# Modulation products of a two-layer attention block: two weight pieces at a time, four chunks of features in four column groups

## The chip, the cores and the metric

One core of one Trainium2 chip runs the whole program. The metric is the time of one execution on the device in microseconds; the kernel before took 3713.2 us, the median of 3 runs (3712.51 to 3716.09).

## The reference, cut to what matters

The reference is two attention layers over 512 tokens and 256 context tokens, followed by two larger blocks (feed-forward, a mixer, cross-attention, feed-forward). Each of the two attention layers scales, shifts and gates its tokens by a modulation, which depends on one vector `c` for the tokens and one, `c_ctx`, for the context:

```python
def _layer(x, ctx, c, c_ctx, w_ada, b_ada, norm_g, w_in, ...):
    mod_x = jax.nn.silu(c) @ w_ada + b_ada
    shift_x, scale_x, gate_x = jnp.split(mod_x[:, None, :], 3, axis=-1)
    mod_c = jax.nn.silu(c_ctx) @ w_ada + b_ada
    shift_c, scale_c, gate_c = jnp.split(mod_c, 3)
    hx = _rmsnorm(x, norm_g) * (1.0 + scale_x) + shift_x
    hc = _rmsnorm(ctx, norm_g) * (1.0 + scale_c) + shift_c
    ...
    x_new = x + gate_x * out_x
```

Here `w_ada` is 1024 x 3072 per layer in float32, and the two vectors are two rows: a product with a large weight (12.6 MB per layer) and almost nothing on the other side.

## The kernel before, in words

**The work as a whole.** `model` (line 1955) runs a start stage, the first block with its two layers (`Block1.run`), and then the second block. Most matrix products are carried in three passes of split weights: `Net.weight` (line 117) loads a piece of 128 x 1024 (512 KB) into a tile `ws`, ScalarE rounds it into `wh` (line 114), VectorE takes the rest into `wl` (line 115), and `mm3` (line 127) issues three matmuls per chunk, on lines 131 to 133. The tiles `wh` come from a ring of four buffers, `whi`.

**The modulation** is `Start.ada`, lines 226 to 258. A layer's 3072 columns are worked in six sixths of 512. For a sixth `g` the 1024 features are eight chunks of 128, which lie in four pieces of the weight with two chunks each. A piece is loaded by SP's queue (line 234) directly into a buffer of the ring `whi`, unsplit, since these products run in plain float32 (two passes per product). Its two products (line 237) follow at once. Each product has the 32 columns of `sT` (of which two, `c` and `c_ctx`, are not zero) as the stationary operand and 512 columns of the weight as the moving one; its 32 output rows lie at `r = 64 * (q % 2) + 32 * k` of one PSUM bank, so that the chunks 0 to 3 go to the four column groups of the array, and chunks 4 to 7 are added to them. ScalarE copies the bank out (line 242); four small matmuls with a selector (line 246) add the four groups and put the features on partitions; VectorE adds the bias (line 248). The function is a generator: it yields after each of the first three pieces, after the copy and after the selector step, five steps per sixth.

**Who calls it, and when.** In `model`, `weave` (line 1964) spreads 20 steps of the first four sixths of layer 0 over 20 rounds, with 10 steps of the memory's keys and values and 20 of the loads of tokens. There the scheduler of the framework places TensorE's instructions. When they are there, `modulated` (line 403) applies scale and shift to the normed tokens, half of the chunks on POOL and half on VectorE (line 418), and the projections of the first unit follow. The other eight sixths (two of layer 0, six of layer 1) are woven into the attention of layer 0: `attend` (line 996) takes one step of `ada` after each block of the attention (line 1021). Two units of neighbourhood attention have 20 blocks each, which makes the 40 steps. The order of TensorE's instructions is that of the code in this part (`manual_schedule`, line 1048). SP's queue issues in order, too: a load that waits for its buffer holds up what stands behind it, such as the exchanged keys `kB` (line 488) and the relative biases `nbase` (line 646).

**What else runs there.** The blocks' own matmuls are scores (lines 493, 494), transposes (722, 552), sums (519) and the preparation of the next head (478). In between comes the fill, `zgate` (line 874), whose two weight pieces stay in use until its last step; `attention` (line 563) spreads its steps over the blocks.

Of the kernel before, what the change touches and what calls it, by code (L numbers as in the profile page):

```python
# [15 lines left out]
P = 128  # L16
# [13 lines left out]
# column ranges of w_in of the first block  # L30
# [3 lines left out]
# column ranges of the table of constants  # L34
# [14 lines left out]
# columns of the packed vectors: vectors of 128 n features as n columns  # L49
# [11 lines left out]
class Net:  # L61
    """Shared pools and building blocks.

    Matrix products with float32 operands are carried by three float32r passes: an operand a is
    hi + lo, hi its rounding to float32r and lo the exact rest, and a*b = hi*hi + hi*lo + lo*hi.
    """
# [12 lines left out]
    # -- allocation ------------------------------------------------------------------------------  # L79
    def psum(self, tag="ps"):  # L80
        """A bank of PSUM; tag: products (ps: p3 and p1), scores (pS), transposes (pT), weighted sums (po), or any (None)."""
        if tag is None:
            tag = ("p3", "pS", "p3", "pT", "p3", "pS", "p1", "po")[self.nps % 8]
            self.nps += 1
        elif tag == "ps":
            tag = ("p3", "p3", "p3", "p1")[self.nprod % 4]
            self.nprod += 1
        return self.pp.tile([P, 512], F32, name=tag, tag=tag, bufs=dict(p3=3, p1=1, pS=2, pT=1, po=1)[tag])
# [4 lines left out]
    # -- constants -------------------------------------------------------------------------------  # L93
# [12 lines left out]
    def bcast_row(self, ap, n, name, pool=None):  # L106
        """A vector of DRAM on every partition."""
        t = (pool or self.cp).tile([P, n], F32, name=name, tag=name)
        self.nc.sync.dma_start(t, ap.partition_broadcast(P))
        return t  # L110

    # -- splitting -------------------------------------------------------------------------------
# [4 lines left out]
    def weight(self, src, nk, eng=None):  # L117
        """A piece of a weight, packed as [128, nk * w], as (hi, lo) of [128, nk, w]."""
# [8 lines left out]
    def mm3(self, pt, items, first=True, last=True):  # L127
        """pt += sum of stationary.T @ moving over items (sh, sl, mh, ml)."""
# [6 lines left out]
    # -- small vectors ---------------------------------------------------------------------------  # L135
# [3 lines left out]
    def rsqrt(self, src, n, mul, add, bufs=3):  # L139
        """1 / sqrt(src * mul + add) of [128, n], by Newton's method."""  # L140
# [17 lines left out]
    def rows(self, r, ts, out, tag="ps"):  # L158
        """out[:, i*128 + t] = r[t, ts[i]] on every partition."""
# [7 lines left out]
def drain(gen):  # L167
    """The rest of a generator."""
    for _ in gen:
        pass  # L170


def during(gen, extra):
    """The steps of a generator, with something more done at some of them."""
    for i, _ in enumerate(gen):
        if extra.get(i):
            extra[i]()
        yield


def weave(gens):
    """Generators in turn, each with its number of steps, spread over the whole."""
# [14 lines left out]
def between(a, b, n):  # L197
    """The steps of a, n of b after each, then the rest of b."""
# [6 lines left out]
class Start:  # L205
    """What does not depend on x: the modulations and the memory's keys and values."""
# [11 lines left out]
    def silu_c(self):  # L218
        net, nc = self.net, self.net.nc
        # c and c_ctx as 2 of 32 columns  # L220
# [5 lines left out]
    def ada(self, l, g0=0, g1=6):  # L226
        """Sixths of the shift, scale and gate of layer l, each with its feature on a partition; a step for each piece of the weight."""
        net, nc = self.net, self.net.nc
        mod, b = self.mod[l], net.col["b_ada"][:, 24 * l:24 * l + 24]
        for g in range(g0, g1):  # L230
            ps = net.psum("p1")
            for q in range(4):
                w = net.whi.tile([P, 1024], F32R, name="wh", tag="wh").bitcast(F32)
                nc.sync.dma_start(w, net.I["w_ada"][l, g, q])
                for k in range(2):
                    r = 64 * (q % 2) + 32 * k
                    nc.tensor.matmul(ps[r:r + 32, :], self.sT[:, 2 * q + k, :], w[:, k * 512:k * 512 + 512],
                                     start=q < 2, stop=q >= 2)
                if q < 3:
                    yield  # L240
# [17 lines left out]
    def memory(self, pool):  # L258
        """The memory with features on partitions and 1/rms of its tokens, on partitions and along rows."""
# [23 lines left out]
    def gained(self, l, hi, lo, mem):  # L283
        """A chunk of the memory times its gains of layer l's norm, as (hi, lo)."""
# [8 lines left out]
    def keys(self, l, hi, lo, put, n):  # L293
        """The memory's keys of layer l; a step for n chunks of features."""
# [12 lines left out]
    def values(self, l, hi, lo, put, n):  # L307
        """The memory's values of layer l; a step for n products of a piece of the weight."""
# [14 lines left out]
    def first(self, pool):  # L323
        """The memory; keys and values of the first layer, in steps."""
# [20 lines left out]
        def normed():  # L345
            """The normed memory, for the second layer."""
# [7 lines left out]
    def second(self, hi, lo, keys, put, n):  # L354
        """Keys or values of the second layer, in steps; hi, lo: four tiles each of 512 columns."""
# [12 lines left out]
class Block1:  # L368
    """Neighbourhood and grouped attention over tokens in the order (column, row), context tokens last."""
# [9 lines left out]
    # -- the modulated norm ----------------------------------------------------------------------  # L379
    def square(self, x, c, acc, pool):  # L380
        """acc += x_c ** 2."""
# [9 lines left out]
    def rms(self, acc, n, pool):  # L391
        """1/rms of each token, along rows."""
# [10 lines left out]
    def modulated(self, xs, l, i, rb=None):  # L403
        """Scale and shift of the normed tokens (i = 0) or of the context (i = 1), as (hi, lo); rb where xs are not normed."""
# [18 lines left out]
    def tok(self, t, pieces, ps, k0=0, k1=8):  # L423
        """ps = hx[token tile t] @ 256 columns, of it the features k0 .. k1."""
# [12 lines left out]
    # -- heads -----------------------------------------------------------------------------------  # L437
    def head_norm(self, ps, out):
        """out = ps / rms of each head of 64; ps and out [128, 2, heads * 64] of two token tiles."""
# [12 lines left out]
    def rope(self, x, nh, t, tabs):  # L452
        """x = x * C + swapped halves of x * S, for token tiles t and t + 1."""
# [12 lines left out]
    def stacked(self, src, nt, name, st):  # L466
        """[hi; lo] on the partitions by tokens, of one head's src [128, nt, 64] (tokens on partitions)."""
# [14 lines left out]
    def keys(self, src, st):  # L482
        """kA: the keys' [hi; lo], kB: its halves exchanged."""
# [12 lines left out]
    def evac(self, dst, src):  # L496
        """A copy out of PSUM, by both engines in turn."""
# [6 lines left out]
    def normed(self, p, sums):  # L504
        """p times half of 1 / sums."""
# [5 lines left out]
    def room(self):  # L511
        """Room for the transposed weights of a pair of query blocks."""
        return self.bq.tile([P, NT * L], F32, name="wT", tag="wT", bufs=2)

    def sums(self, ps, parts):
        """ps[0:64] + ps[64:128] = sum of V.T @ weights over parts (V, weights), keys on partitions."""
# [4 lines left out]
    def result(self, ps, i, at, o):  # L521
        """The sums of head i of a unit, to its rows of o."""
# [5 lines left out]
    def ctx_queries(self, st, keys, vs, i, n, o):  # L528
        """Stages of the context queries, on the context keys alone."""
# [33 lines left out]
    def attention(self, heads, fill, done, lag, steps, last):  # L563
        """A unit's heads, each (its preparation, its blocks), the first prepared.

        The transposes of a block's weights come lag steps after its scores, its sums one more; the preparation of the
        next head and the fill run in between.
        """
# [3 lines left out]
        # steps of the fill after each block, more of them where nothing is prepared  # L572
# [25 lines left out]
    # -- neighbourhood attention -----------------------------------------------------------------  # L598
    def bank(self):
        """Banks of the projections in turn."""  # L600
# [3 lines left out]
    def na_proj(self, l, u, out):  # L604
        """Keys, queries and values of four heads; a step for each token tile."""
# [7 lines left out]
        def pairs(w, ts, dst, gain=None):  # L613
            """The normed heads of token tiles, two at a time."""
# [26 lines left out]
    def na_base(self, l, u):  # L641
        """Relative biases of four heads: query (cq, rq) on a partition, key (j, rk)."""
# [7 lines left out]
    def na_bias(self, base):  # L650
        """Negated relative bias, for the first, the inner and the last query blocks, then zeros for the context."""
# [11 lines left out]
    def unit_out(self):  # L663
        """The tile of a unit's heads, there from its first use on."""
# [8 lines left out]
    def na_unit(self, l, u, d):  # L673
        """The heads of a unit and what is left to do after them."""
# [6 lines left out]
    def na_head(self, l, i, nq, d, base, o):  # L681
# [26 lines left out]
        def parts(b):  # L708
            """(columns of the weights, V) of the block's keys, 128 at a time, then 64."""
# [34 lines left out]
    # -- grouped attention -----------------------------------------------------------------------  # L744
    def gqa_tables(self, l):
        """Rotary tables with the gains, for queries (with the negated scale) and keys."""
# [19 lines left out]
    def normed_rope(self, ps, nh, t, n, x):  # L766
        """The normed and turned heads of token tiles t and t + 1."""
# [9 lines left out]
    def gqa_proj(self, l, g, out):  # L777
        """Queries of four heads and, of both groups, keys and values; a step for each token tile."""
# [30 lines left out]
    def gqa_unit(self, l, g, d):  # L809
        """The heads of a unit and what is left to do after them."""  # L810
# [58 lines left out]
    # -- gates, output, residual -----------------------------------------------------------------  # L869
    def units(self, d, l, u):  # L870
        """Unit u of a layer's scratch in DRAM: [128, 256 * token tiles]."""
        return d[l].rearrange("p (u c) -> p u c", u=4)[:, u, :256 * (NT if l == 0 else 4)]

    def zgate(self, l, u):
        """z * (1 + tanh(z / 2)), twice silu(z), of a unit; four steps for a token tile."""
# [22 lines left out]
    def gate(self, l, u, o, z):  # L898
        """The unit's attention times its gate, to DRAM."""
# [5 lines left out]
    def early_gate(self, l, j):  # L905
        """Chunk j of the gates, to DRAM; a step for each chunk of features."""
# [13 lines left out]
    def gated(self, l, u, n_):  # L920
        """The unit's gated attention with features on partitions: two chunks of (hi, lo)."""
# [1195 lines left out]
```

## Time and profile before

| | |
|---|---|
| median of 3 runs | 3713.2 us (3712.51 to 3716.09) |
| span of the profiled execution | 3715.2 us |
| TensorE matmul busy | 3618.4 us, 97% |
| TensorE weight loads busy | 2996.4 us, 81% |
| VectorE, ScalarE, GpSimd busy | 2070.7, 1375.2, 762.7 us |
| moved by DMA | 364.35 MB, mean 98 GB/s |
| loads of the modulation weight | 48 of 512 KB |

The profile is one execution. PE stands for TensorE's matmuls, PEld for its weight loads, DVE, ACT, POOL and SP (SPq: its queue) for the vector, scalar, GpSimd and sync engines. An entry such as `L237` is a line of the kernel; `p<-wh,sT` names the tile written and the tiles read. Matmuls are pipelined, so the duration of one overlaps the next; the distance between starts tells what an instruction holds up. A bracket at the end of a timeline row is the time that the engine was idle before it, and what ended the wait. Times count from the start of the span.

### The profile page before, as it was taken

To read this page: it belongs to the slowest core of one execution; us is meant where nothing else is said; L and a number is where in the kernel's file an instruction comes from. 1 tells how busy PE (TensorE), PEld (TensorE's weight loads), DVE (VectorE), ACT (ScalarE), POOL (GpSimd) and SP (SyncE) were. 2 spreads that over 40 slices of the span, in tenths; PEclk is the share of its full clock that TensorE was granted. 3 is DMA by queue.
4 is the path that set the end of the run, shared out by engine and by line. 5 is a ranking of instruction groups with operands and counts; after the bars stand their busy time and mean duration, and the time that the engine had idled before them with its cause. 6 is when DMAs were issued, how large, how long until landed. Compare 5 with 4: busy or idle time off the path is not lost.

```text
span 3715.2 us, 51467 instructions
## 1 busy us (share of the span) xinstructions
PE 3618.4 (97%) x19706; PEld 2996.4 (81%) x19706; DVE 2070.7 (56%) x4209; ACT 1375.2 (37%) x2407; POOL 762.7 (21%) x908
## 2 busy tenths in 40 slices
PE   8999999999999999999999999999999999999998
PEld 6887778888887778888778888888888888788887
DVE  6665763376566464334766433443347887664335
ACT  4334443233345432223654322322233333443223
POOL 1222330032233011102320100210025444101001
PEclk9999999999999999999999999999999999999999
DMA  8434113143322333333122333333333212322333
GB/s 276 128 111 136 58 49 128 63 142 88 88 70 67 139 100 102 97 94 105 58 91 63 108 97 97 97 97 97 97 100 112 57 56 74 115 75 93 101 98 103
DMA packets 135718, 364.35 MB, mean 98 GB/s; under 512 B 30000, under 2 KB 43184, under 8 KB 134960
## 3 DMA queue, kind: packets, MB, share of 16 engines
q1 hardware_dynamic: 135472, 361.06, 31.2%
q8 instruction: 155, 2.54, 0.3%
q14 instruction: 91, 0.75, 0.1%
HBM read 331.64 MB, written 19.66 MB: 95 GB/s over the span
## 4 chain that ended last, share of the span: by engine, by line
PE 87%; DVE 6%; ACT 2%; DMA 2%; issue 1%; POOL 1%; SPq 0%; DVEq 0%; ACTq 0%; POOLq 0%
PE p L131 15%; PE p L133 15%; PE p L132 15%; PE pS L131 7%; PE pS L132 6%; PE pS L133 6%; PE po L519 2%; PE pT L132 2%; PE pT L131 2%; PE pT L133 2%; PE po L132 2%; PE po L131 2%; PE po L133 2%; DVE wl L115 1%; PE pS L493 1%
## 5 line engine op out<-in xcount | busy, mean ns | idle before, releaser
L114 ACT ACTIVATE wh<-ws 128x1024 fp32r<-128x1024 f32 (+4 forms) x561 | 563.7, 1006 | 1421.8 <-PE p L132 683.8
L115 DVE TENSOR_TENSOR wl<-ws,wh 128x1024 fp32r<-128x1024 f32 (+3 forms) x542 | 640.4, 1182 | 252.7 <-ACT wh L114 250.8
L131 PE MATMUL p<-nh,wh 128*128 128x512 f32 x1084 | 429.1, 397 | 4.5 <-ACT nh L1132 2.0
L133 PE MATMUL p<-nh,wl 128*128 128x512 f32 x1084 | 424.7, 392 | 4.7 <-DVE wl L115 4.7
L132 PE MATMUL p<-nl,wh 128*128 128x512 f32 x1084 | 424.2, 391 | 1.9 <-DVE nl L115 1.9
L1199 POOL TENSOR_TENSOR g<-g,rb 128x512 f32<-128x512 f32 x88 | 149.8, 1704 | 1137.1 <-ACT g L1198 1137.1
L131 PE MATMUL pS<-nh,wh 128*128 128x512 f32 x620 | 254.5, 411 | 1.0 <-DVE xr L1182 1.0
L133 PEld LDWEIGHTS p<-nh,wl 128*128 128x128 f32 x1084 | 203.5, 188 | 50.3 <-DVE wl L115 6.2
L133 PE MATMUL pS<-nh,wl 128*128 128x512 f32 x620 | 242.8, 392 | 0.0
L132 PE MATMUL pS<-nl,wh 128*128 128x512 f32 x620 | 242.6, 391 | 0.0
L131 PEld LDWEIGHTS p<-nh,wh 128*128 128x128 f32 x1084 | 203.6, 188 | 46.8 <-ACT nh L1132 2.5
L132 PEld LDWEIGHTS p<-nl,wh 128*128 128x128 f32 x1084 | 203.7, 188 | 42.2 <-DVE nl L115 2.2
L1197 DVE TENSOR_TENSOR g<-p,rb 128x512 f32<-128x512 f32 x88 | 60.4, 691 | 227.8 <-PE p L133 217.6
L131 PE MATMUL p<-hxh,wh 128*128 128x512 f32 (+1 forms) x456 | 183.9, 403 | 0.8 <-DVE wT L502 0.8
L132 PE MATMUL p<-hl,wh 128*128 128x512 f32 (+1 forms) x488 | 179.8, 369 | 0.0
L133 PE MATMUL p<-hh,wl 128*128 128x512 f32 (+1 forms) x488 | 179.4, 368 | 0.0
L131 PE MATMUL p<-hh,wh 128*128 128x512 f32 (+1 forms) x488 | 179.3, 368 | 0.0
L1141 POOL TENSOR_TENSOR acc<-acc,sq 128x512 f32<-128x512 f32 x48 | 73.5, 1532 | 477.4 <-ACT sq L1140 477.0
L133 PE MATMUL p<-hxh,wl 128*128 128x512 f32 (+1 forms) x456 | 170.5, 374 | 0.0
L132 PE MATMUL p<-hxl,wh 128*128 128x512 f32 (+1 forms) x456 | 170.5, 374 | 0.0
L509 POOL TENSOR_SCALAR p<-p,rinv 128x768 f32<-128x768 f32 (+2 forms) x128 | 104.3, 815 | 254.0 <-DVE rinv L508 145.7
L1212 DVE SCALAR_TENSOR_TENSOR xr<-p,xr 128x512 f32<-128x512 f32 (+1 forms) x68 | 42.5, 627 | 170.0 <-PE p L133 169.9
(592 smaller groups left out, 8864.2 us busy)
## 6 DMA issues: line engine op xcount, KB each, us to landing
ws<-in_ffn_w_in_dram SPq DMA_DIRECT2D x176, 512.0 KB
ws<-in_ffn_w_out_dram SPq DMA_DIRECT2D x64, 512.0 KB
ws<-in_w_in_tok_dram SPq DMA_DIRECT2D x52, 512.0 KB
wh<-in_w_ada_dram SPq DMA_DIRECT2D x48, 512.0 KB
ws<-in_ffn_w_out_dram SPq DMA_DIRECT2D x40, 384.0 KB
ws<-in_w_out_dram SPq DMA_DIRECT2D x24, 512.0 KB
ws<-in_dn_qkv_dram SPq DMA_DIRECT2D x24, 512.0 KB
ws<-in_xa_wk_dram SPq DMA_DIRECT2D x16, 512.0 KB
```

Of the source, the lines that this page charges most:

```text
L114: self.last_hi = self.nc.scalar.activation(hi, src, AF.Copy)
L115: (eng or self.nc.vector).tensor_tensor(out=lo, in0=src, in1=hi.bitcast(F32), op=OP.subtract)
L131: mm(pt, sh, mh, start=first and i == 0, stop=False)
L132: mm(pt, sh, ml, start=False, stop=False)
L133: mm(pt, sl, mh, start=False, stop=last and i == n - 1)
L493: mm(ps, q, kA[:, k0:k1], start=True, stop=False)
L509: nc.gpsimd.tensor_scalar(p, p, r, 0.5, op0=OP.mult, op1=OP.mult)
L519: self.net.nc.tensor.matmul(ps[h:h + HD, :], v, w, start=i < 2, stop=i >= len(parts) - 2)
L1141: (nc.vector if c == 7 else nc.gpsimd).tensor_tensor(out=acc, in0=acc, in1=sq, op=OP.add)
L1197: nc.vector.tensor_tensor(t, pg, self.rb, op=OP.mult)
L1199: nc.gpsimd.tensor_tensor(out=t, in0=t, in1=self.rb, op=OP.mult)
L1212: nc.vector.scalar_tensor_tensor(x, ps, 0.5, x, op0=OP.mult, op1=OP.add)
```

## The change

The loop over the four pieces of a sixth becomes one over two halves. A half takes two buffers of the ring, loads two pieces, and issues its four products one behind the other, each to a column group of its own. A sixth has three steps where it had five, and the number of steps in the start stage's `weave` follows. All other lines differ only in comments.

```diff
         for g in range(g0, g1):
             ps = net.psum("p1")
-            for q in range(4):
-                w = net.whi.tile([P, 1024], F32R, name="wh", tag="wh").bitcast(F32)
-                nc.sync.dma_start(w, net.I["w_ada"][l, g, q])
-                for k in range(2):
-                    r = 64 * (q % 2) + 32 * k
-                    nc.tensor.matmul(ps[r:r + 32, :], self.sT[:, 2 * q + k, :], w[:, k * 512:k * 512 + 512],
-                                     start=q < 2, stop=q >= 2)
-                if q < 3:
+            for h in range(2):
+                ws = []
+                for q in (2 * h, 2 * h + 1):
+                    ws.append(net.whi.tile([P, 1024], F32R, name="wh", tag="wh").bitcast(F32))
+                    nc.sync.dma_start(ws[-1], net.I["w_ada"][l, g, q])
+
+                for i in range(4):
+                    nc.tensor.matmul(ps[32 * i:32 * i + 32, :], self.sT[:, 4 * h + i, :],
+                                     ws[i // 2][:, i % 2 * 512:i % 2 * 512 + 512], start=h == 0, stop=h == 1)
+                if h == 0:
                     yield
             y = net.sm.tile([P, 512], F32, name="yada", tag="yada", bufs=1)
             nc.scalar.activation(y, ps, AF.Copy)
...
-            drain(weave([(st.ada(0, 0, 4), 20), (chain(keys, islice(values, 2)), 10), (b1.first(pool), 20)]))
+            drain(weave([(st.ada(0, 0, 4), 12), (chain(keys, islice(values, 2)), 10), (b1.first(pool), 20)]))
```

## Rows read from the trace of the kernel before

**Rows 1.** The page: the span, and TensorE's busy time, share, instructions.
```profile
span 3715.2 us, 51467 instructions
PE 3618.4 (97%) x19706; PEld 2996.4 (81%) x19706; DVE 2070.7 (56%) x4209; ACT 1375.2 (37%) x2407; POOL 762.7 (21%) x908
```

**Rows 2.** The line of the modulation products: duration min/median/max in ns, first and last start.
```profile
L237 PE MATMUL p<-wh,sT x192: 592/605/1061, 13.2 to 353.9; 128*32 128x512 f32 x192
```

**Rows 3.** Windows (length, busy us and instructions per engine, PEclk, DMA share, GB/s).
```profile
10.00:30.00 20.00, 18.18 (x100) 14.23 (x101) 12.52 (x31) 10.98 (x21) 0.00 (x0) 1.00 1.00 376
...
160.00:226.00 66.00, 65.05 (x458) 42.57 (x456) 39.09 (x107) 34.57 (x82) 25.56 (x46) 1.00 0.53 154
...
292.00:358.00 66.00, 64.82 (x459) 42.45 (x458) 39.14 (x106) 33.36 (x83) 21.89 (x40) 1.00 0.50 146
```

**Rows 4.** Timeline of TensorE in the first attention stretch (start, duration, line, tiles).
```profile
162.42 1.05 PE L237 MATMUL p<-wh,sT 128*32 128x512 f32 x4
...
177.76 1.05 PE L237 MATMUL p<-wh,sT 128*32 128x512 f32 x4
178.74 0.38 PE L493 MATMUL pS<-kA,qA 128*128 128x256 f32 x1
...
181.35 1.05 PE L237 MATMUL p<-wh,sT 128*32 128x512 f32 x4
...
222.08 1.05 PE L237 MATMUL p<-wh,sT 128*32 128x512 f32 x4
```

**Rows 5.** Timeline of TensorE in the start stage, where visits stand together.
```profile
53.18 1.06 PE L237 MATMUL p<-wh,sT 128*32 128x512 f32 x8
54.18 0.39 PE L131 MATMUL p<-mh,wh 128*128 128x256 f32 x1
...
66.05 1.91 PE L237 MATMUL p<-wh,sT 128*32 128x512 f32 x12
```

**Rows 6.** Timeline of SP's queue: loads of the modulation weight, and kB's transfers.
```profile
166.07 0.33 SPq L234 DMA_DIRECT2D wh<-in_w_ada_dram  x1
...
178.85 0.33 SPq L234 DMA_DIRECT2D wh<-in_w_ada_dram  x1
...
297.24 0.33 SPq L234 DMA_DIRECT2D wh<-in_w_ada_dram  x1
297.67 1.11 SPq L488 DMA_DIRECT2D kB<-kA  x2
```

**Rows 7.** Waits of SP's queue, 155 to 230 us: total, times, longest.
```profile
SPq L234 <- PE p L237: 30.4, 10, 7.9
```

**Rows 8.** Timeline of TensorE: visits that waited for their load.
```profile
171.01 1.05 PE L237 MATMUL p<-wh,sT 128*32 128x512 f32 x4 [0.87 <-DMA wh<-in_w_ada_dram]
...
302.41 1.05 PE L237 MATMUL p<-wh,sT 128*32 128x512 f32 x4 [1.10 <-DMA wh<-in_w_ada_dram]
```

**Rows 9.** Two 512 KB loads alone: SP's queue, then windows (last two columns: DMA).
```profile
2830.20 0.81 SPq L121 DMA_DIRECT2D ws<-in_dn_qkv_dram  x2
...
2833.00:2834.00 1.00, 0.01 (x1) 0.01 (x1) 0.84 (x2) 0.12 (x1) 0.88 (x3) 1.00 0.99 406
...
2834.30:2834.60 0.30, 0.30 (x5) 0.30 (x4) 0.24 (x1) 0.00 (x0) 0.22 (x2) 1.00 0.17 68
2834.60:2835.00 0.40, 0.40 (x4) 0.31 (x3) 0.31 (x1) 0.00 (x0) 0.32 (x2) 1.00 0.00 0
```

**Rows 10.** Waits of TensorE in layer 1's neighbourhood attention, 880 to 1060 us.
```profile
PE pS L494 <- DMA kB<-kA: 7.8, 4, 2.4
```

**Rows 11.** A gap on TensorE in layer 1, and the window behind it.
```profile
890.88 0.33 PE L494 MATMUL pS<-kB,qA 128*128 128x192 f32 x1 [1.74 <-DMA kB<-kA]
...
891.30:894.60 3.30, 3.30 (x13) 2.62 (x11) 0.80 (x3) 1.69 (x3) 1.49 (x3) 0.50 0.03 5
```

**Rows 12.** The end of the start stage: POOL's scaling, TensorE's first projection.
```profile
83.59 12.51 POOL L418 TENSOR_SCALAR x<-x,modA,mod 128x512 f32<-128x512 f32 x8
...
98.48 0.58 PE L131 MATMUL pS<-wh,hxh 128*128 128x256 f32 x1 [6.59 <-ACT vo L342]
```

## The prediction

> **What bounds the kernel now.** I read the page first: matmuls are busy 97% of the span [rows 1], so a microsecond taken from TensorE is worth a microsecond wherever it does not have to wait for something else there. The change touches only the modulation products, so I asked next where those stand. The line of their matmuls has 192 records between 13.2 and 353.9 us [rows 2]. In the timeline they come in groups of four records (two products, each two passes), so there are 48 visits: four for each of 12 sixths, 16 of them in the start stage (to about 74 us) and 32 in the neighbourhood attention of the first layer, in two stretches of 16. In those two stretches TensorE is busy 65.05 and 64.82 of 66 us [rows 3]: there it is the bound, and it works in the order in which the code lists its instructions. In the start stage it shares that place with the loads: from 10 to 30 us the DMA engines are busy without a pause at 376 GB/s [rows 3]. Third, I looked at what happens around one visit, on TensorE and on the queue that issues its loads.
>
> **What the change takes away.** A visit holds TensorE from 177.76 to 178.74, 0.98 us to the start of the next instruction [rows 4]. Whether four column groups really run at once need not be guessed: at 53.18 us two visits with different column groups happen to stand together, eight records, and the next instruction starts at 54.18, after 1.00 us [rows 5]. So the second pair of column groups is free, and each merged visit saves one whole visit. Twelve records that fall on the same groups again took 1.91 us [rows 5], so the saving needs different groups, which the new loop gives. Attention: 16 visits go, and with 0.06 us each for the slower first instruction behind a visit that is 16 x 1.04 = 16.6 us. Start stage: 8 go, of which two were already merged with a neighbour in rows 5, so 6 x 1.04 = 6.2 us at most. The eviction, the small products with the selector and the DVE additions are as many as before: nothing.
>
> **What it adds: the loads lose their lead.** A visit's piece goes into a buffer of the ring of four that the split weights also use. In the attention stretches two of the four hold the two pieces of z's weight until the stretch is nearly over (the fill runs through every block), so two are left. The trace shows that they are all there is: the load issued at 178.85 goes out 1.09 us after the visit that began at 177.76, when its buffer came free [rows 4, 6], and the queue spent 30.4 us in one stretch, 10 times, waiting for these matmuls [rows 7]. Now one piece is loaded while the other is used, so a load has two visits' time to arrive. After the change a visit uses both buffers; neither load of the next visit can go out before this one is over.
>
> How long until a pair is there? One 512 KB piece that shared the DMA engines with the two kB transfers (384 KB) was issued at 166.07 and used at 171.01, with TensorE idle 0.87 us for it: 4.94 us; likewise from 297.24 to 302.41, 5.17 us with 1.10 us of idling [rows 6, 8]. Two 512 KB pieces alone, issued at 2830.20, move until between 2834.3 and 2834.6, 4.1 to 4.4 us [rows 9], and a semaphore has to follow. I take 4.9 us, with 4.2 and 5.9 as the ends (the quiet pair; a pair beside kB, longer by the 1 us that its 384 KB take at the pair's 406 GB/s). With the 1.09 us before the issue, the next merged visit can start 6.0 us after this one did.
>
> How long does TensorE have other work? The events of a stretch (visit or selector step, one after each block) run from 162.42 to 222.08 in 18 intervals, 3.31 us each [rows 4]. After the change the steps of a sixth are visit, visit, selector. From the second visit to the next sixth's first are two intervals, 6.6 us: hidden, save beside kB. From the first to the second is one, 3.3 us: 6.0 - 3.3 = 2.7 us idle. Eight sixths stand in the attention: 8 x 2.7 = 21.6 us (ends 8 x 2.0 = 16 and 8 x 3.7 = 30). TensorE's order there is fixed by hand, so nothing slips into the gap. The two waits of rows 8, 2.0 us, fall away, since this count covers them.
>
> The Trainium skill (Trainium Kernel Development and Optimization, section Best Practices) asks to double-buffer so that DMA and compute overlap, and that speaks against this change, which fills both buffers at once. By that rule alone every one of the 16 merged visits would wait; by the intervals just counted only every second one does, because the selector step gives the other pair its time. I keep the count from the intervals.
>
> **What moves.** The attention has 24 steps of modulation instead of 40, so the work ends four blocks into the second stretch. The first stretch keeps 14 merged visits and its idle time; the second loses nearly all of its 16. Does TensorE then find something to wait for there? Layer 1 runs the same heads without modulation: it waited 7.8 us, 4 times, for kB [rows 10]. The first layer has one block more per head, so I charge 2 us (0 to 6). On SP's queue the kB transfers and the 16 bias loads now stand between paired loads: 2 us more (0 to 5).
>
> **Clock.** After an idle 1.74 us at 890.88 the granted clock was 0.50 from 891.3 to 894.6, the 1.2 GHz level [rows 11]: 3.3 us at half speed lose up to 1.65 us. The new gaps are as long, but each is broken by the half visit whose piece lands first. I charge it at half of the eight gaps, 4 x 1.5 = 6 us (0 to 13).
>
> **Start stage.** 6.2 us go from TensorE, but the stage ends by another chain: the scaling on POOL, 12.51 us from 83.59, after which TensorE starts the projections at 98.48 with 6.59 us of idling [rows 12]. That chain hangs on the modulation and on the keys, both of which finish sooner; on the other side the first pair is 1 MB ahead of the first keys' weight in a full queue (about 1.4 us at 376 GB/s). I take -4 us (-12, if POOL's chain moves up too, to +5).
>
> **Sum.** -16.6 - 2.0 + 21.6 + 2 + 2 + 6 - 4 = +9.0. Against the profiled execution's 3715.2 us that is 3724; that execution lies 2.0 us over the median of the runs, 3713.2, so the forecast is 3722 us, 0.24% slower. I call 0.2%, 7.4 us, the least that a measurement can tell from no change.
>
> **Rivals.**
> - *The loads stay hidden; not slower.* Place: the second visit of each sixth in the attention. Price: if a pair is there 4.6 us after the previous visit's start instead of 6.0, the idle time is 1.3 us a sixth, 10.4 us in all, no gap is long enough to touch the clock, and the sum is -18.6 + 10.4 + 2 - 4 = -10: 3703; with a third buffer free it is -18.6 - 6 = -25: 3689. It decides from about 2 us a sixth downwards. For it: the visits' saving is sure. Against it: rows 6 and 7 show two buffers, rows 9 a pair that moves for 4.1 us.
> - *A wash.* Idle time of 2.2 us a sixth (17.6 us) and no lower clock: -18.6 + 17.6 + 4 - 4 = -1: 3712. It asks only for small errors of two terms.
> - *The clock falls after each gap, and the start gains nothing.* +9 + 7 + 4 = +20: 3733. For it: rows 11; against it: the gaps are broken by half visits.
> - *The four products don't run at once.* Then nothing is saved at all and the idle time stays; the row at 53.18 speaks against it.
>
> **How the numbers follow.** Exposed loads as summed 0.36, with the clock after each gap 0.09, a wash 0.28, hidden 0.25, no concurrency 0.02. The first case's own spread reaches down to no change, and a wash reaches a little over the bound on either side: slower 0.42, same 0.34, faster 0.24. The range goes from the better half of the hidden case, 3692, to the clock case with a few microseconds for the unknown ends, 3737.
>
> **What would show it.** In the changed profile: visits of eight records in about 1.05 us; idle time in front of the modulation line put down to the load of the modulation weight, some 15 to 22 us in about eight places, all in the first stretch save one; pairs of loads issued 0.4 us apart, each just behind a visit; the second stretch shorter by some 12 us and the first longer by as much or more; half-clock stretches between 160 and 230 us. The prediction is wrong if that idle time is below 10 us, or if single loads still run a visit ahead.

## The result, and the profile after

The changed kernel takes 3744.1 us (median of 4 runs, 3742.29 to 3746.08) against 3714.6 (4 runs, 3712.51 to 3718.15): ratio 1.0079, 95% interval 1.0065 to 1.0093, 29.5 us slower. The forecast was 3722, its range ended at 3737. The sign was right, the size and the range were not. The page of the kernel after, as [rows 1]:

```profile
span 3744.3 us, 51467 instructions
PE 3619.7 (97%) x19706; PEld 2997.6 (80%) x19706; DVE 2074.8 (55%) x4209; ACT 1375.8 (37%) x2407; POOL 768.2 (21%) x908
```

TensorE is busy 1.3 us more than before while the span is 29.1 us longer: nearly the whole loss is idle time on TensorE. Where? I paired the matmuls that both kernels issue (same line, tiles and shape, in order; the modulation's own left out) and took how much later each starts in the new trace. The median of the matmuls that start within the next few microseconds of some times of the old trace, in us:

| time in the old trace | 20 | 40 | 70 | 80 | 100 | 155 | 225 | 285 | 305 | 345 | 365 | 400 | 3700 |
|---|---|---|---|---|---|---|---|---|---|---|---|---|---|
| changed kernel later by | 4.0 | 6.6 | 6.7 | 15.1 | 12.9 | 13.5 | 36.1 | 36.1 | 40.6 | 29.3 | 27.9 | 29.0 | 29.5 |

Two places make nearly all of it. The start stage loses 13.5 us. The two attention stretches lose 22.6 (13.5 to 36.1) and give 8.2 back (36.1 to 27.9), so 14.4, or 15.5 if the 29.0 of 400 us is taken. Afterwards the difference stays at 29 to 30.

**Attention.** Windows of the kernel after, as [rows 3] (length, busy us and instructions per engine, PEclk, DMA share, GB/s):

```profile
10.00:30.00 20.00, 18.00 (x85) 13.82 (x84) 10.61 (x28) 9.64 (x18) 0.00 (x0) 1.00 0.91 345
160.00:226.00 66.00, 57.16 (x375) 38.44 (x376) 26.32 (x71) 22.02 (x54) 14.28 (x27) 0.95 0.51 162
```

TensorE fell from 65.05 to 57.16 busy microseconds in the first stretch's window. Its waits between 155 and 400 us (total, times, longest), all that the view lists for the engine:

```profile
PE p L239 <- DMA wh<-in_w_ada_dram: 16.9, 12, 3.7
PE po L521 <- DVE o L528: 1.8, 2, 1.5
```

The visits themselves, in the timeline of TensorE of the kernel after:

```profile
175.87 1.07 PE L239 MATMUL p<-wh,sT 128*32 128x512 f32 x8
180.72 1.05 PE L239 MATMUL p<-wh,sT 128*32 128x512 f32 x4 [2.20 <-DMA wh<-in_w_ada_dram]
182.83 1.59 PE L239 MATMUL p<-wh,sT 128*32 128x512 f32 x4 [1.06 <-DMA wh<-in_w_ada_dram]
...
189.18 1.06 PE L239 MATMUL p<-wh,sT 128*32 128x512 f32 x8
194.03 1.05 PE L239 MATMUL p<-wh,sT 128*32 128x512 f32 x4 [1.04 <-DMA wh<-in_w_ada_dram]
195.34 1.05 PE L239 MATMUL p<-wh,sT 128*32 128x512 f32 x4 [0.27 <-DMA wh<-in_w_ada_dram]
...
207.41 3.29 PE L239 MATMUL p<-wh,sT 128*32 128x512 f32 x8 [2.34 <-DMA wh<-in_w_ada_dram]
...
338.14 3.23 PE L239 MATMUL p<-wh,sT 128*32 128x512 f32 x8 [3.71 <-DMA wh<-in_w_ada_dram]
```

The first visit of a sixth (175.87, 189.18) has its pair ready and does eight records in 1.06 us. The second (180.72, 194.03) waits for its first piece, does half, waits again and does the other half: the two halves, 1.05 us each, are not merged, so such a visit saves nothing. Five of the eight second visits are split like this; the other three (207.41, 338.14 and one at 261.02, which has no bracket and takes 1.88 us) wait for their second piece inside the visit, two of them at half clock. The loads, in the timeline of SP's queue, as [rows 6]:

```profile
176.97 0.81 SPq L236 DMA_DIRECT2D wh<-in_w_ada_dram  x2
179.01 1.11 SPq L490 DMA_DIRECT2D kB<-kA  x2
```

The pair goes out 1.10 us after the visit at 175.87 began, two loads 0.4 us apart. Its first piece is used at 180.72, its second at 182.83: 3.75 and 5.86 us after the issue. Behind the waits the clock falls; windows of the kernel after on three stretches (same columns, PEclk is the third number from the end):

```profile
183.20:186.60 3.40, 3.40 (x11) 2.02 (x8) 0.70 (x2) 0.85 (x2) 0.14 (x1) 0.50 0.77 232
207.10:210.50 3.40, 3.08 (x8) 0.38 (x8) 0.00 (x0) 0.00 (x0) 0.00 (x0) 0.50 0.32 98
336.80:343.60 6.80, 5.46 (x19) 2.65 (x20) 2.27 (x4) 2.80 (x4) 0.33 (x1) 0.50 0.29 105
```

They are granted 0.50, the 1.2 GHz level, during or after waits of 2.20 (with one of 1.06 close behind it), 2.34 and 3.71 us. Behind the other waits (1.76 us at most) it stayed at 1.00, though in [rows 11] it had fallen behind 1.74 us.

**Start stage.** TensorE's two long waits there, as the last row of [rows 12]; the kernel before had 0.17 and 6.59 us at the same two matmuls:

```profile
93.94 0.80 PE L131 MATMUL pS<-wh,mh 128*128 128x512 f32 x1 [8.93 <-ACT vo L344]
...
111.99 0.58 PE L131 MATMUL pS<-wh,hxh 128*128 128x256 f32 x1 [4.81 <-ACT vo L344]
```

With the 6.7 us that the stage is late by at 70 us, the sum is 6.7 + (8.93 - 0.17) + (4.81 - 6.59) = 13.7, close to the 13.5 measured (smaller differences are left out). The first wait names `vo`, the values that ScalarE copies out. So I read ScalarE's timeline, first of the kernel before:

```profile
79.71 1.25 ACT L342 ACTIVATE vo<-pS,mr 128x512 f32<-128x512 f32 x2
82.31 1.07 ACT L114 ACTIVATE wh<-ws 128x1024 fp32r<-128x1024 f32 x1 [1.35 <-DMA ws<-in_xa_wv_dram]
83.28 0.61 ACT L114 ACTIVATE hxh<-x 128x512 fp32r<-128x512 f32 x1
```

and of the kernel after:

```profile
79.41 1.07 ACT L114 ACTIVATE wh<-ws 128x1024 fp32r<-128x1024 f32 x1 [6.34 <-DMA ws<-in_xa_wv_dram]
80.38 4.57 ACT L114 ACTIVATE hxh<-x 128x512 fp32r<-128x512 f32 x9
84.86 1.04 ACT L114 ACTIVATE wh<-ws 128x1024 fp32r<-128x1024 f32 x1
85.81 0.70 ACT L114 ACTIVATE hxh<-x 128x256 fp32r<-128x256 f32 x2
87.52 0.72 ACT L114 ACTIVATE hxh<-x 128x256 fp32r<-128x256 f32 x2 [1.01 <-POOL x L420]
89.80 0.72 ACT L114 ACTIVATE hxh<-x 128x256 fp32r<-128x256 f32 x2 [1.55 <-POOL x L420]
91.00 0.42 ACT L114 ACTIVATE hxh<-x 128x256 fp32r<-128x256 f32 x1 [0.48 <-POOL x L420]
91.32 1.99 ACT L114 ACTIVATE wh<-ws 128x1024 fp32r<-128x1024 f32 x2
93.22 1.25 ACT L344 ACTIVATE vo<-pS,mr 128x512 f32<-128x512 f32 x2
```

Before, the first values were out (79.71) before ScalarE began to split the scaled tokens (`hxh`). After, sixteen of these splits stand ahead of the values: three of the values' weight splits (`wh`) come only at 84.86 and 91.32, and `hxh` waits in between for POOL's scaling. SP's queue is held too, as its timeline in the kernel after shows: after 82.42 (78.93 + 3.49) it issues nothing until the store of `ko` at 91.85, and the next piece of the values' weight stands behind that store.

```profile
78.93 3.49 SPq L121 DMA_DIRECT2D ws<-in_xa_wv_dram  x2
91.85 4.87 SPq L352 DMA_DIRECT2D md<-ko  x4
96.81 0.38 SPq L121 DMA_DIRECT2D ws<-in_xa_wv_dram  x1
```

POOL's timeline explains the store. Before, all eight `ko` were ahead of its scaling; the last is this row, and the scaling of [rows 12] follows it at 83.59:

```profile
82.68 0.93 POOL L349 TENSOR_TENSOR ko<-memT,mrb 128x256 f32<-128x256 f32 x1 [2.54 <-DMA md<-ko]
```

In the kernel after, four of the eight come behind the scaling (two of them here):

```profile
78.48 12.49 POOL L420 TENSOR_SCALAR x<-x,modA,mod 128x512 f32<-128x512 f32 x8
90.93 1.76 POOL L351 TENSOR_TENSOR ko<-memT,mrb 128x256 f32<-128x256 f32 x2
```

So the scaling did start 5.1 us sooner than before (78.48 instead of 83.59), and the stage ended 13.5 us later.

### The profile page after: what moved, and what is told of

Read it like the earlier page. It is cut to its first block, busy times and chain, and to the rows that moved or that the text cites. A ratio compares the mean times of both kernels' runs of the same rounds, so it can differ in the third digit from the quotient of the medians.

```text
span 3744.3 us, 51467 instructions
## 1 busy us (share of the span) xinstructions
PE 3619.7 (97%) x19706; PEld 2997.6 (80%) x19706; DVE 2074.8 (55%) x4209; ACT 1375.8 (37%) x2407; POOL 768.2 (21%) x908
## 4 chain that ended last, share of the span: by engine, by line
PE 86%; DVE 6%; DMA 3%; ACT 2%; issue 1%; POOL 1%; SPq 0%; DVEq 0%; ACTq 0%; POOLq 0%
PE p L131 15%; PE p L133 15%; PE p L132 15%; PE pS L131 7%; PE pS L132 6%; PE pS L133 6%; PE po L521 2%; PE pT L132 2%; PE pT L131 2%; PE pT L133 2%; PE po L131 2%; PE po L132 2%; PE po L133 2%; DMA wh<-in_w_ada_dram 1%; DVE wl L115 1%
## 5 line engine op out<-in xcount | busy, mean ns | idle before, releaser
L133 PEld LDWEIGHTS pS<-nh,wl 128*128 128x128 f32 x620 | 116.5, 188 | 25.4
```

Of the source, the lines that this page charges most:

```text
L133: mm(pt, sl, mh, start=False, stop=last and i == n - 1)
```

## The experiments

After the result I held this theory: two separate losses, one in each place; in the attention too little time between a pair's issue and its use, in the start stage an in-order queue (ScalarE's, SP's or POOL's) on which the scaled tokens' work was moved ahead of the values'. Rivals are named with the runs. A ratio is against the kernel before, run on the same chip (medians 3715.4, 3715.5 and 3714.8 in the three groups); "later" is the table's quantity, at the end of the start stage (100 us) and behind the attention (400 us).

| kernel | pairs in | us (runs) | ratio, 95% interval | later at 100 | later at 400 |
|---|---|---|---|---|---|
| att_single | start | 3725.4 (7) | 1.0029, 1.0018 to 1.0040 | 12.3 | 12.9 |
| start_single | attention | 3731.2 (4) | 1.0040, 1.0025 to 1.0055 | 1.4 | 15.0 |
| mdq_pairs_in_start | start | 3724.0 (10) | 1.0025, 1.0015 to 1.0034 | 7.0 | 7.8 |
| pool_order | start | 3729.0 (5) | 1.0036, 1.0023 to 1.0049 | 11.4 | 13.1 |
| act_order | start | 3715.2 (10) | 0.9998, 0.9988 to 1.0007 | 1.2 | 3.1 |
| act_order_mdq | start | 3716.1 (10) | 1.0001, 0.9991 to 1.0011 | 0.4 | 0.6 |
| after_act_only | both | 3730.8 (4) | 1.0044, 1.0028 to 1.0059 | 0.9 | 19.5 |
| spaced_attention | attention | 3709.7 (10) | 0.9986, 0.9977 to 0.9995 | 0.7 | -2.0 |
| spaced2_attention | attention | 3705.7 (9) | 0.9975, 0.9965 to 0.9984 | 1.5 | -7.5 |
| spaced2_act_pairs | both | 3708.9 (11) | 0.9984, 0.9975 to 0.9993 | 6.0 | -3.3 |
| spaced2_act_single | attention | 3703.9 (7) | 0.9969, 0.9958 to 0.9980 | 2.3 | -4.7 |

Behind 400 us single profiles drift apart by up to 7 us in work that the edits don't touch (spaced_attention is at -2.0 at 400 us and at -9.4 at 3700), so I compare places by the last two columns and kernels by the ratio.

**Half of the change each.** In these two kernels one caller takes the old function (called `ada_single`), the other the new one.

First att_single, then start_single:

```diff
-        ada = chain(self.start.ada(0, 4, 6), self.start.ada(1, 0, 6)) if l == 0 else iter(())
+        ada = chain(self.start.ada_single(0, 4, 6), self.start.ada_single(1, 0, 6)) if l == 0 else iter(())
```

```diff
-            drain(weave([(st.ada(0, 0, 4), 12), (chain(keys, islice(values, 2)), 10), (b1.first(pool), 20)]))
+            drain(weave([(st.ada_single(0, 0, 4), 20), (chain(keys, islice(values, 2)), 10), (b1.first(pool), 20)]))
```

> Start stage as changed (pairs), attention as before (one piece at a time). The shift of equal matmuls between the two profiles was +13.5 us at the end of the start stage. Theory (two separate losses that add): the start's +13.5 stays and the attention's goes, 3714.6 + 13.5 = 3728 us. Rival (the start's delay is only a shift that a saturated attention would absorb or the attention's loss follows from the later start): 3715 to 3720 or over 3735.

> Start stage as before, attention as changed. Theory: only the attention's loss is left, +22.7 in the first stretch and -7 in the second, 3714.6 + 15.6 = 3730 us, with about 17 us of TensorE idling in front of the modulation products for their loads. Rival as for the run before: if the two losses don't add, well off 3730.

Measured: 10.0 and 15.8 us slower. The first is late by 12.3 us at the start's end and by nothing more in the attention; the second the other way round, with 14.3 us of waits for the modulation's weight on TensorE. Together that is 25.8 us against the 29.5 of the whole change, the same within the intervals: the losses are separate.

**The start: which queue?** Three edits on att_single. The first moves the stores of `ko` from SP's queue to POOL's, so that no weight stands behind them:

```diff
-                nc.sync.dma_start(self.md[:, c * L:(c + 1) * L], o)
+                nc.gpsimd.dma_start(self.md[:, c * L:(c + 1) * L], o)
```

> As the first run (pairs in the start stage alone), but the eight stores of the normed memory are issued by POOL's queue instead of SP's. Theory: in the changed profile SP's queue issues nothing from 82.1 to 91.9 us, since a store stands at its head whose tile POOL makes only after the scaling; with the stores off that queue the weights of the values and of the projections are loaded in time, and at least 9 of the 13.5 us come back: 3714 to 3719 us. Rival (the pairs themselves delay the start: 1 MB ahead of the first keys' weight, visits split in two): the +13.5 stays, about 3728 us.

Measured: only 5.3 of the 12.3 us come back. The second long wait is gone from TensorE's timeline, the first is still there (timeline of mdq_pairs_in_start):

```profile
93.44 0.79 PE L131 MATMUL pS<-wh,mh 128*128 128x512 f32 x1 [10.70 <-ACT vo L365]
```

The second edit makes POOL finish all eight `ko` before its scaling; it also moves the code of the scaled tokens behind that of the values:

```diff
-                nc.gpsimd.tensor_tensor(out=o, in0=self.mem[c], in1=self.mrb, op=OP.mult)
+                self.last_ko = nc.gpsimd.tensor_tensor(out=o, in0=self.mem[c], in1=self.mrb, op=OP.mult)
...
-            b1.h = [b1.modulated(b1.x0[i], 0, i) for i in range(2)]
             drain(chain(values, normed))
+            with tc.issue_after(st.last_ko.ins):
+                b1.h = [b1.modulated(b1.x0[i], 0, i) for i in range(2)]
```

> Pairs in the start stage alone, but POOL makes all eight tiles of the normed memory before the scaling, as the kernel before did. Theory (the order on POOL started both blockings): the shift at the end of the start stage goes back to 0 to +4. Rival: +12 stays.

Measured: 11.4 us late, nothing regained, and TensorE waits 12.12 us. In ScalarE's timeline the splits of the scaled tokens still stand between the values' weight splits and now wait even longer for POOL:

```profile
82.39 1.06 ACT L114 ACTIVATE wh<-ws 128x1024 fp32r<-128x1024 f32 x1 [1.10 <-DMA ws<-in_xa_wv_dram]
87.40 1.15 ACT L114 ACTIVATE hxh<-x 128x512 fp32r<-128x512 f32 x2 [3.95 <-POOL x L441]
88.46 1.04 ACT L114 ACTIVATE wh<-ws 128x1024 fp32r<-128x1024 f32 x1
```

So neither POOL's order decides nor putting the values' code first. The third edit orders ScalarE: the work on the scaled tokens is issued there behind the split of the last values' weight (`last_hi`). The code of `normed`, which makes and stores the `ko`, moves behind the scaled tokens with it.

```diff
-            b1.h = [b1.modulated(b1.x0[i], 0, i) for i in range(2)]
-            drain(chain(values, normed))
+            drain(values)
+            with tc.issue_after(net.last_hi.ins):
+                b1.h = [b1.modulated(b1.x0[i], 0, i) for i in range(2)]
+            drain(normed)
```

> Pairs in the start stage alone (as att_single, +12.3 us at the end of the start stage, 1.0029 of before), but the 16 splits of the scaled tokens are placed on ScalarE behind the last split of a values' weight. In att_single those splits stand on ScalarE's queue ahead of the splits of two values' weights, and wait there for POOL's 12.3 us of scaling, while TensorE idles 9.0 us for the weights. Theory (ScalarE's queue is blocked by the scaling, which the new schedule moved up): the gap of 9 us shrinks to under 3, the gap of 4.9 us behind SP's blocked queue stays or grows by a few us: shift at the end of the start stage +3 to +8. Rival (the weights themselves come late because of the pairs' loads): the gap stays, +12.

Measured: 3715.2 us, no different from the kernel before, 1.2 us late at 100 us. ScalarE's timeline in act_order:

```profile
86.94 1.06 ACT L114 ACTIVATE wh<-ws 128x1024 fp32r<-128x1024 f32 x1 [3.84 <-DMA ws<-in_xa_wv_dram]
87.91 1.25 ACT L365 ACTIVATE vo<-pS,mr 128x512 f32<-128x512 f32 x2
89.05 1.06 ACT L114 ACTIVATE wh<-ws 128x1024 fp32r<-128x1024 f32 x1
89.99 6.72 ACT L114 ACTIVATE hxh<-x 128x512 fp32r<-128x512 f32 x16
```

and TensorE's:

```profile
88.63 0.50 PE L131 MATMUL pS<-wh,mh 128*128 128x512 f32 x1 [1.89 <-ACT vo L365]
101.60 0.39 PE L131 MATMUL pS<-wh,hxh 128*128 128x256 f32 x1 [1.51 <-ACT vo L365]
```

All sixteen splits now stand in one row behind the weights, and the waits of 8.99 and 4.87 us became 1.89 and 1.51. I had expected the second to stay, for SP's queue, and a shift of 3 to 8 us. It went, because the same edit changed SP's order, too, as SP's timeline in act_order shows: the last weights of the values go out ahead of the stores that had stood before them.

```profile
77.08 7.59 SPq L121 DMA_DIRECT2D ws<-in_xa_wv_dram  x3
86.27 1.01 SPq L373 DMA_DIRECT2D md<-ko  x2
```

POOL is as in att_single: four `ko` ahead of the scaling, which starts at 76.41, and four behind. So the first wait is ScalarE's order: it stayed with the stores off SP's queue (10.70 us) and with POOL's order mended (12.12), and went when ScalarE's was. The second is SP's: it is gone in all three kernels, and in all three no weight of the values stands behind a store that waits for the scaling. With SP's queue alone mended 7.0 of the 12.3 us are left; ScalarE's order alone, with SP's as it was, no kernel here shows. Adding the stores' move to this kernel tests whether SP's queue still holds something:

> The run before with, besides, the stores of the normed memory on POOL's queue, which alone took 5.3 us off the shift. Theory (two blocked queues, ScalarE's and SP's, both because POOL scales earlier; nothing else lost): both gaps go, the shift at the end of the start stage is between -5 and +2, the whole 3710 to 3717 us. Rival (the early part, where visits are split and TensorE is 2 to 5 us behind at 40 to 70 us, is lost too): +4 to +7.

Measured: the same time within the intervals. Nothing more is left for SP, and nothing is gained by the pairs in the start stage either.

**The attention: time between issue and use.** The stretch has 40 blocks and the pairs need 24 steps, so there is room for empty steps. Both kernels have the old start stage; spaced_attention takes one empty step between the two visits of a sixth, as below, and spaced2_attention two (the added `yield` twice).

```diff
-        ada = chain(self.start.ada(0, 4, 6), self.start.ada(1, 0, 6)) if l == 0 else iter(())
+        ada = chain(self.start.ada(0, 4, 6, True), self.start.ada(1, 0, 6, True)) if l == 0 else iter(())
...
                 if h == 0:
                     yield
+                    if spare:
+                        yield
```

> Start stage as before; in the attention pairs as changed, but with an empty step between the first and the second visit of a sixth, so that four steps make a sixth and each pair has two steps, 6.6 us, to arrive. Theory (two free buffers, so that a pair's loads go out only behind the visit before, and one step is too short for them): the idling for the modulation weight falls from 17 us to under 4, both visits of a sixth merge, and the saving of 16 visits shows: 3714.6 - 10 to -17, 3698 to 3705 us. Rival (the products of four column groups, or the emptier second stretch, cost the time): stays near 3730.

Measured: 3709.7, a little outside the expectation. The waits fell to 5.2 us. Second visits of spaced_attention mostly come 4.8 to 5.7 us behind the first now, and that is still just short:

```profile
176.36 1.06 PE L239 MATMUL p<-wh,sT 128*32 128x512 f32 x8
182.08 1.75 PE L239 MATMUL p<-wh,sT 128*32 128x512 f32 x8
```

At 182.08, 5.7 us behind the first, the second piece came while the visit ran: 1.75 us instead of 1.06. With two empty steps:

> Start stage as before, pairs in the attention with two empty steps between the first and the second visit of a sixth, so that there are three blocks between them and the 40 steps end where they ended before. With one empty step the second visits still came 5.2 to 5.7 us behind the first, before the second piece (6.0 us), and ran in two halves; 3709.7 us. Theory (a pair needs 6.0 us from visit to visit): no visit waits, all 16 are merged, 16 x 1.04 = 16.6 us go: 3699 to 3704 us. Rival (what the merged visits save comes back as waits for the attention's own work): no better than 3708.

Measured: 3705.7 us, just above the expectation, and faster than the kernel before. TensorE's waits for these loads between 155 and 400 us are 1.4 us, two in number. What still keeps it from the full 16.6 us of the visits is in part what the rival named: over the work up to 400 us TensorE is busy 12.4 us less than before, but waits 4.5 us for VectorE's `o` where it waited 0.3. The rest is in the visits of spaced2_attention:

```profile
169.24 1.05 PE L239 MATMUL p<-wh,sT 128*32 128x512 f32 x4
170.93 1.05 PE L239 MATMUL p<-wh,sT 128*32 128x512 f32 x4 [0.64 <-DMA wh<-in_w_ada_dram]
177.67 1.06 PE L239 MATMUL p<-wh,sT 128*32 128x512 f32 x8
...
186.38 1.06 PE L239 MATMUL p<-wh,sT 128*32 128x512 f32 x8
192.43 1.77 PE L239 MATMUL p<-wh,sT 128*32 128x512 f32 x8
```

From 177.67 to 186.38 (8.7 us) a pair has time; from 186.38 to 192.43 (6.05 us, two steps) it just hasn't, 0.7 us more. With 40 steps for eight sixths not both gaps can be three steps long. A fifth buffer in the ring might free the loads earlier; that wasn't tried.

**Do the parts add?** Three last kernels: the changed kernel with ScalarE's order mended and nothing else, and both mends together with either start stage.

> The changed kernel, with one edit: on ScalarE the splits of the scaled tokens are issued behind the split of the last values' weight. If the change's 29.5 us are two separate losses, some 13.5 in the start stage through ScalarE's order and some 15.6 in the attention through exposed loads, this kernel keeps only the second: 3731 us (3728 to 3734), shift of the same matmuls about +1 at 100 us and +15 to +17 at 400 us. If the loss in the attention depends on what the start leaves behind, the sum fails: below 3726 or above 3737.

Measured: 3730.8, late by 0.9 us at 100 and 19.5 at 400 us. The median is the expected one; the profiled execution lies 2.5 us above the 15 to 17 at 400 us.

> Paired visits in both places, with ScalarE's order mended in the start stage and two empty steps between the two visits of a sixth in the attention. Theory that the two parts simply add: 0 to +1 us from the start and -7 to -10 from the attention, 3706 to 3709 us, slightly behind single visits in the start. Rival: the pairs' 6 us saved on TensorE in the start come through once ScalarE's order is mended, 3699 to 3703 us.

Measured: 3708.9, 0.16% faster than the kernel before; the rival fails again: the pairs in the start bring nothing. Its profile is 6.0 us late at 100 us, where after_act_only, with the same code in the start, is late by 0.9; TensorE's last wait for `vo` there is 4.04 us against 1.60. Why is open, so in this kernel the start's part doesn't simply add.

> Single visits in the start stage as in the kernel before, ScalarE's order mended, two empty steps in the attention. If ScalarE's order costs nothing when the visits are single (in the kernel before the scaling came late enough), this equals the kernel with the empty steps alone: 3704 to 3707 us. If the same blocking also costs the kernel before a part of its 6.59 us of idling there, 3699 to 3702 us.

Measured: 3703.9, 0.31% faster than the kernel before and 1.1% faster than the changed one; the best of all kernels here. Its interval overlaps that of spaced2_attention, and it is 2.3 us late at 100 us, so no gain from ScalarE's order is seen where the start has single visits. Of its 11 us the profile places 4.7 in front of 400 us.

## Why the prediction was right and wrong

**The failed step is the start stage, "I take -4 us (-12, if POOL's chain moves up too, to +5)": it measured +13.5.** I followed one chain, POOL's scaling to the first projection, and argued that what feeds it finishes sooner. It did, by 5.1 us. But the bracket of the last row in [rows 12] named `vo`, the values from ScalarE, and I read past it. In this stage the framework's scheduler places the instructions, so a change in one engine's work can change every other queue's order. ScalarE got sixteen splits ahead of the values' weights, and TensorE stood for 8.93 us; SP's queue held the values' last weight behind a store, and TensorE stood for 4.81 more (6.59 before). That these two orders cost it is shown (act_order, which mends both: 12.3 to 1.2; with SP's alone 7.0 are left). That the scheduler chose it because the modulation looked ready sooner is only argued. The other half of my reasoning, six visits saved, failed too: of the sixteen halves of the start's visits twelve stand alone in TensorE's timeline, presumably since the scheduler places each when it expects its piece to be there. And the loads of the keys' weights went out later (the second at 11.21 instead of 9.23 us), while from 10 to 30 us the DMA engines moved 345 GB/s instead of 376: that the stage is 6.7 us late at 70 us fits this, but I didn't take it apart. In act_order (8.4 us late at 70) a later wait absorbs it: 1.51 us where the kernel before had 6.59.

**The attention was right in its mechanism and close in size: +13 forecast with the clock, 14.4 to 15.5 measured.** The waits stand at seven of the eight second visits, six of them in the first stretch; the eighth, at 261.02, waits only inside. Of the terms:

- Idle time: 21.6 us forecast, 16.9 measured, inside the 15 to 22 given. It is smaller because a half visit begins 4.85 us after the previous visit (175.87 to 180.72, 189.18 to 194.03), when the first piece is there; the whole pair is in use only after 6.2 to 7.0 us in these rows, where I had 6.0.
- What I missed: that half visit is then not merged. Five split visits give back 5 x 1.04 = 5.2 us of the 16.6, and four visits of eight records take 1.63, 1.88, 3.23 and 3.29 us instead of 1.06, 5.8 us more. I had written that the half visit breaks the gap, and not that this is paid for.
- kB and SP's queue: 4 us charged, no such wait in the view; a wait of `po` for VectorE (1.8 us, 0.3 before) came instead, 3.2 us if the new trace is read to 429 us, where the work of the old 400 us ends.
- Clock: 6 us charged; three stretches of 13.6 us at 0.50, in which TensorE was busy 11.9, cost up to 6.0 (by my estimate about 2.6 of it already in the long visits).
- Together: -16.6 + 5.2 + 5.8 + 16.9 - 2.0 + 1.5 + 3.4 = 14.2; with 2.9 for `po` instead of 1.5 it is 15.6, for the 15.5 at 400 us.
- The second stretch gave back 8.2 us, not some 12: its one second visit waited 3.71 us.
- A single load ran a visit ahead once, in the last pair of the first stretch: its loads went out at 253.03 and 258.36, before and after the visit at 257.27 began.

The page of the Trainium skill that I weighed (Trainium Kernel Development and Optimization, Best Practices: double-buffer so that loads and compute overlap) points the right way. By it alone all 16 visits would have waited; in the trace TensorE's waits stand in front of second visits only, at seven of the eight, so the count from the intervals stands (one first visit, at 242.37, waited inside for its second piece and took 1.63 us).

**The rivals.** The nearest was the clock after each gap with no gain in the start, 3733; its start term was still 13.5 us short. Hidden loads came true only when the visits were moved apart (3705.7; that the sum worked out for that rival was 3703 is luck, since it holds 10.4 us of idle time and a gain of 4 us in the start, which this kernel doesn't have). The range was too narrow in one term alone: I had bounded the start's loss at 5 us without a row that shows what a scheduler may rearrange.

## What to carry to other kernels

Merging two users of a double buffer into one halved TensorE's time for them here (1.06 us instead of twice 1.05) and took the loads' lead away: count the time from the previous use to the next one against the time that the whole pair needs, and if there are spare steps, put them there; here two empty steps turned a loss of 15 us behind the attention into a gain of 7.5. Where a scheduler orders the queues, a step that is ready sooner can be put ahead of work that the critical engine needs; compare each queue's order, not only the times. The releaser that a row's bracket names is the chain to follow first.

## What I had not expected of the hardware

Two 512 KB loads issued 0.4 us apart beside other traffic don't come together: the first piece was used 3.75 us after the pair's issue, the second after 5.86 (with kB behind it), and 1.31 us lay between the halves at 194.03 and 195.34. Products to four column groups that stand together run in 1.06 us, but with a late second piece each half costs the full 1.05.
